# Transposes of a mixer unit's output: offered to later chain steps instead of issued when due

## The chip, the cores and the metric

The kernel runs on one core of a Trainium2 chip. Its time is the device time of one launch in microseconds (us); of several runs the median is given. The engines named here are TensorE (PE in the profile, with its weight loads as PEld), VectorE (DVE), ScalarE (ACT), GpSimd (POOL) and SyncE (SP, which issues most DMAs). Each works through its own instructions in order and waits for the others by semaphores. A matmul writes to PSUM, and VectorE or ScalarE bring its result from there to SBUF.

## The reference

One decoder layer on a sequence of 2048 tokens with 1024 channels: a token mixer with three kinds of heads, then a gated MLP with a short convolution. Cut to what matters here:

```python
def token_mixer(h, w_in, ...):
    proj = h @ w_in
    o_r = retention_chunkwise(rotary(q), rotary(k), v, log_gamma)      # 4 heads
    o_h = gated_state_chunkwise(silu(hq), key_h, hi, log_f)            # 8 heads
    o_a = gated_state_chunkwise(aq, ak, av, g_log)                     # 4 heads
    # each: per-head RMSNorm, times silu of a gate
    o = concatenate([o_r, o_h, o_a]) * head_gain
    return o @ w_out

x = x + g1 * token_mixer(rms_norm(x) * (1 + sc1) + sh1, ...)
x = x + g2 * conv_ffn(rms_norm(x) * (1 + sc2) + sh2, ...)
return rms_norm(x) * final_gain
```

The recurrences are computed by chunks: scores inside a chunk, and a state that is carried from chunk to chunk.

## The kernel before

**Blocks and units.** The sequence is cut into 4 blocks of 512 tokens. In each block the mixer works through 7 units (`ORDER`, L34): h0, g, h1, h2, h3, r0, r1. An h unit is two HGRN2 heads, g is the four GLA heads (it gives two outputs, "first" and "second" below), an r unit is two retention heads. A unit begins with big products that project its inputs (`cf_gemm`, `tf_gemm`, `tf512`). Each is a product in three parts (`split3`, L290): operands are split into a high and a low piece, and three matmuls of up to 512 columns make one step. They fill most of TensorE's time. After that comes the unit's **chain**, a line of small steps, each of which needs what VectorE and ScalarE made of the one before.

**The chain of an h or g unit** (`gated`, L713): dots and the levels 0 and 1 of a tree of scores (L801 to L807), then levels 2 and 3, 4 and 5, and at last 6 alone. Between two pairs the decays are multiplied into q and k (`faded`, on VectorE) and copies are made of them (`ahead`, on ScalarE: `qc`, `kc`). Then: a transpose of k (`kT`, L834), the state's update (`u`, L845), the attention's output (`attn_out`, L857), its normalization and gate (`post`, L639), and, `POST_GAP` (21 us) later, the output's transposes (`transposed`, L652). These are four 128x128 transposes of the unit's output `o` into one PSUM buffer, which ScalarE (L660, the high part) and VectorE (L661, the low part) then read into a tile `oT` for the output projection. For g's second output the gap is 3 us. The chain of a retention unit (`retention`, L988): transposes of q and k and the state's update, scores (L1012 to L1016), the attention's output, the same normalization and transposes.

**What sets the order.** TensorE's order is written out by hand (`manual_schedule`): it is the order in which the Python program emits its instructions. The chains are woven into the big products by a planner (`Clock`, L60), which has a model time `t`. Each emitted product adds its modelled time (`adv`); when `t` passes the due time of a chain's step, that step is emitted at this place. A chain's generator yields the gap in us to its next step; `yield None` lets the next unit's chain begin. `until(done)` (L97) runs due steps one after another, and moves `t` up to their due times, until a condition holds. The program calls it where it can't go on without a result: at L1301, after the first unit of a block, until all eight `oT` of the block before exist, ahead of the second half of that block's output projection (`out_finish`, whose products are `y`); at L1307 for the first four `oT`; and at the mixer's end (L1318, L1322). VectorE's, ScalarE's and SyncE's order is left to a scheduler at build time, by priorities and the order of the program.

**Riders.** A step may yield a pair of times instead of a gap, `(soon, late)` (`RIDE`, L56). From `soon` on it is offered as a rider; the next step that calls `clock.pick()` (L82) emits all riders on offer right behind itself; if none came by `late`, the step is emitted then. Before the change `u` and the attention's output of h and g units and the first part of the statistics for the next block's norm ride. Riders are picked behind the levels 2 and 3, 4 and 5, and 6 (L825), and nowhere else.

**PSUM and SBUF.** Two PSUM buffers, `late_ps` (L155), serve in turn for the dots, `kT`, `u`, the attention's output, `oT` and the norm's statistics (`rstd`). The tiles `a4k` (8 buffers) hold the `oT` and the score matrices; `room(n)` (L231) holds a step back, 1 us at a time, until the planner counts n of them free.

Of the kernel before, what the change touches and what calls it, by code (L numbers as in the profile page):

```python
# [53 lines left out]
FIRST_GAP = 8.0  # L54
PAIR_GAP = (5.2, 6.4)
RIDE = (2.4, 7.4), (3.8, 9.0)  # L56
STAT_GAP, STAT_LAND, NORM_GAP = 2.4, 3.0, 2.0


class Clock:  # L60
# [31 lines left out]
    def adv(self, us):  # L92
        self.t += us
        while self.due and self.due[0][0] <= self.t:
            self._next()
# [29 lines left out]
def trunk(ctx, tc, xT, vecs, cvec, cst, rope, msk, wada, win, walow, wgla, wout, wup, wdown, out):  # L125
# [13 lines left out]
    clock = Clock()  # L139
# [5 lines left out]
    def lev_ps(name):  # L145
        return pp.tile([P, 512], F32, tag="lev", name=name, bufs=2)

    def tiled(out, lhs, rhs, start=True, stop=True):

        for g in range(0, P, 32):  # L150
            T.matmul(out[g:g + 32], lhs[:, g:g + 32], rhs(g) if callable(rhs) else rhs, start=start, stop=stop)
# [3 lines left out]
    def late_ps(name):  # L155
        return pp.tile([P, 512], F32, tag="late", name=name, bufs=2)
# [74 lines left out]
    def room(n):  # L231

        while held[0] + n > NA4:
            yield 1.0
        held[0] += n
# [403 lines left out]
    def post(o, sg, name):  # L639

        o8 = o[:].rearrange("p c (h e) -> p (c h) e", e=64)
        sq = late("osq" + name)
        S.activation(sq[:], o[:].rearrange("p c e -> p (c e)"), AF.Square)
        ms = small("oms" + name)
        V.tensor_reduce(ms[:], sq[:].rearrange("p (a e) -> p a e", e=64), axis=mybir.AxisListType.X, op=ALU.add)
        V.tensor_scalar(ms[:], ms[:], 1.0 / 64, EPS, op0=ALU.mult, op1=ALU.add)
        rs = small("ors" + name)
        newton(ms, rs, 8)
        V.tensor_tensor(o8, o8, rs[:].unsqueeze(2).to_broadcast([P, 8, 64]), op=ALU.mult)
        marked(V.tensor_tensor(o[:], o[:], sg[:], op=ALU.mult))  # L650

    def transposed(b, pos, o, name):  # L652

        ps = late_ps("oT" + name)
        for c in range(NCH):
            T.transpose(ps[:, c * P:(c + 1) * P], o[:, c, :], ident)
        oT = pa.tile([P, 2, TB], F32R, tag="a4k", name="oT" + name)
        g = vec[:, V_HG + pos:V_HG + pos + 1]
        with tc.high_priority(offset=CHAIN):
            S.activation(oT[:, 0, :], ps[:], AF.Copy, scale=g)  # L660
            V.scalar_tensor_tensor(oT[:, 1, :], ps[:], g, oT[:, 0, :], op0=ALU.mult, op1=ALU.subtract)  # L661
        oTs[b][pos] = oT

    def attn_out(name, b, attn, v, qn, W):


        ps = late_ps("o" + name)
        for c in range(NCH):
            oc = ps[:, c * P:(c + 1) * P]
            inter = not (b == 0 and c == 0)  # L670
            if inter:
                tiled(oc, qn[:, c * P:(c + 1) * P], W[:, c, :], stop=False)
            for hh in range(2):
                at, col = attn[hh]
                tiled(oc[:, hh * 64:hh * 64 + 64], at[:, (c * 2 + col) * P:(c * 2 + col + 1) * P],
                      v[:, c, hh * 64:hh * 64 + 64], start=not inter, stop=hh == 1 or not inter)
        return ps

    def carry(b, Sst, ps, decay):

        W = wide.pop(0)
        wide.append(W)
        at = pu.tile([P, NCH - 1, 64], F32, tag="Sc", name="Sc", bufs=2)
        halves = slice(0, 64), slice(64, P)
        if b:
            for rs in halves:
                S.copy(W[rs, 0, rs], Sst[rs, :])
        for c in range(NCH):
            last = c == NCH - 1
            dst, u = Sst[:] if last else at[:, c, :], ps[:, c * 64:c * 64 + 64]  # L690
            if b == 0 and c == 0:
                V.tensor_copy(dst, u)
            elif not last or b < NB - 1:
                V.scalar_tensor_tensor(dst, at[:, c - 1, :] if c else Sst[:], decay(c), u, op0=ALU.mult, op1=ALU.add)
        for rs in halves:
            S.copy(W[rs, 1:NCH, rs], at[rs, :, :])
        return W
# [15 lines left out]
    def gated(name, b, ui, pos, kq, q, decay, subs, qk, sel):  # L713
# [127 lines left out]
        adv(MT)  # L841
        yield RIDE[0]
        ps = late_ps("u" + name)
# [5 lines left out]
        adv(ML)  # L849
        yield RIDE[1]  # L850
        os = []
        for i, (rows, v, sg) in enumerate(subs):
            if i:
                yield RIDE[1]
            o = pu.tile([P, NCH, P], F32, tag="o", name=f"o{name}_{i}")
# [9 lines left out]
        for i, o in enumerate(os):  # L865
            yield POST_GAP if i == 0 else 3.0
            yield from room(1)
            transposed(b, pos + i, o, f"{name}_{i}")
            adv(MT)

# [40 lines left out]
    def unit_g(b, pos):  # L911
# [32 lines left out]
        for i in range(2):  # L944
            rows = [(32 * i, 32 * i + 32), (64 + 32 * i, 96 + 32 * i)]
            for r0, r1 in rows:
                S.copy(q[r0:r1, i, :], qs[r0:r1, :])
            subs.append((rows, *tok_tiles(f"{nm}_{i}")))
        clock.chain(gated(nm, b, 4, pos, kq, q, decay, subs, qk, selg), 12.5)
        pss = tf512(f"vg{nm}", 18)  # L950
        for i in range(2):
# [4 lines left out]
    def unit_r(b, r, pos):  # L956
# [16 lines left out]
        for x, y in zip(a, bb):  # L973
# [10 lines left out]
                        a[1][:].rearrange("p (c h n) -> p c h n", c=NCH, n=64),  # L984
                        kd.unsqueeze(1).unsqueeze(3).to_broadcast([P, NCH, 2, 64]), op=ALU.mult)
        clock.chain(retention(nm, b, r, pos, a[0], kk, kc, q, vsg), 14.5 if b < 3 else 11.0)

    def retention(nm, b, r, pos, a, kk, kc, q, vsg):  # L988
        v, sg = vsg
        Sst = states[5 + r]  # L990
        gc = c_all[:, C_GC + r:C_GC + r + 1]
        qps, kps = lev_ps("qT" + nm), lev_ps("kT" + nm)
        for c in range(NCH):
            T.transpose(qps[:, c * P:(c + 1) * P], a[:, c * P:(c + 1) * P], ident)
        for c in range(NCH):
            T.transpose(kps[:, c * P:(c + 1) * P], kk[:, c, :], ident)
        qn = pu.tile([P, TB], F32, tag="f", name="qn" + nm, bufs=3)
        with tc.high_priority(offset=CHAIN):
            S.copy(kc[:], kps[:])
            S.copy(q[:, 0, :], qps[:])  # L1000
            S.activation(qn[:], qps[:], AF.Copy, scale=gc)
        ps = late_ps("u" + nm)
        for c in range(NCH):
            tiled(ps[:, c * 64:c * 64 + 64], kk[:, c, :], lambda g: v[:, c, g // 64 * 64:g // 64 * 64 + 64])
        with tc.high_priority(offset=CHAIN):
            W = carry(b, Sst, ps, lambda c: gc)
        adv(2 * MT + ML)
        yield 3.5
        yield from room(1)
        at = pa.tile([P, 8 * P], F32, tag="a4k", name="at" + nm)  # L1010
        pss = [lev_ps(f"sc{nm}_{hh}") for hh in range(2)]
        for c in range(NCH):  # L1012
            for g in range(0, P, 32):
                for ps, r0 in zip(pss, (0, 64)):
                    T.matmul(ps[g:g + 32, c * P:(c + 1) * P], kc[r0:r0 + 64, c * P + g:c * P + g + 32],
                             q[r0:r0 + 64, 0, c * P:(c + 1) * P], start=True, stop=True)  # L1016
        with tc.high_priority(offset=CHAIN):
            for hh, ps in enumerate(pss):
                V.tensor_tensor(at[:].rearrange("p (c h n) -> p c h n", c=NCH, h=2)[:, :, hh, :],
                                ps[:].rearrange("p (c n) -> p c n", n=P),  # L1020
                                causal.unsqueeze(1).to_broadcast([P, NCH, P]), op=ALU.mult)
        adv(MS)
        yield 3.0
        ps = attn_out(nm, b, [(at, hh) for hh in range(2)], v, qn, W)
        o = pu.tile([P, NCH, P], F32, tag="o", name="o" + nm)
        qd = c_all[:, C_QD + 2 * r:C_QD + 2 * r + 2]
        with tc.high_priority(offset=CHAIN):
            V.tensor_tensor(o[:].rearrange("p c (h e) -> p c h e", e=64),
                            ps[:].rearrange("p (c h e) -> p c h e", h=2, e=64),
                            qd.unsqueeze(1).unsqueeze(3).to_broadcast([P, NCH, 2, 64]), op=ALU.mult)  # L1030
        with tc.high_priority(offset=AFTER):
            post(o, sg, nm)
        held[0] -= 1
        adv(MO)
        yield None
        yield POST_GAP
        yield from room(1)
        transposed(b, pos, o, nm)
        adv(MT)

# [776 lines left out]
```

## Time and profile before

| | us |
|---|---|
| median of 3 runs (2408.58 to 2411.97) | 2409.89 |
| span of the profiled execution, from its first to its last instruction | 2407.7 |
| TensorE's mean granted clock in it | 0.997 |

The page gives the span of the profiled execution, not its launch time; the runs' median is 2.2 us longer. The mixer's blocks end at about 284, 558, 830 and 1133 us, and the MLP follows to the end.

The output's transposes are 128 matmuls on line 656, in 32 groups of four. Their starts, from the timeline of TensorE, and behind each the start of the next levels 2 to 6 or retention score step on TensorE (us; "behind" says that the group stands right behind another small step):

| unit | block 0 | block 1 | block 2 | block 3 |
|---|---|---|---|---|
| h0 | 138.95, behind a pair of levels | 377.00, 382.26 | 650.58, 654.54 | 922.61, 926.56 |
| g first | 179.37, 181.33 | 451.11, behind o; 458.99 | 725.83, behind o; 733.22 | 997.36, behind o; 1003.38 |
| g second | 183.43, 202.65 | 456.97, 475.07 | 731.21, 748.61 | 1001.42, 1018.50 |
| h1 | 197.98, 202.65 | 476.56, 481.20 | 750.10, 754.74 | 1019.99, 1024.63 |
| h2 | 228.53, 248.76 | 506.49, 521.00 | 780.03, 794.53 | 1049.02, 1057.95 |
| h3 | 266.89, 277.18 | 539.50, 549.29 | 812.86, 822.65 | 1081.31, 1088.08 |
| r0 | 283.59, behind o; 315.09 | 557.24, behind o; 588.73 | 823.74, behind the score | 1086.85, 1088.08 |
| r1 | 305.81, 315.09 | 579.45, 588.73 | 851.48, 860.75 | 1108.43, none |

Here "o" is an attention's output. How a timeline row is read: start in us from the span's beginning, duration, engine, line, operation, output <- inputs by the program's names, shape, and how many instructions were merged; in brackets the idle time before it and what ended it. Matmuls are pipelined, so durations overlap: what an instruction costs is read from starts.

### The profile page before, as it was taken

Reading aid. Unit: us, or ns where it says so; the run is one execution under the profiler, and the core shown is the slowest. Engines: PE = TensorE matmul, PEld = TensorE weight load, DVE = VectorE, ACT = ScalarE, POOL = GpSimd, SP = SyncE. Lnnn points to the kernel's source line nnn. Section 1 sums busy time; section 2 is a strip of 40 time slices with the busy share of each in tenths; the row PEclk is TensorE's granted clock in tenths of the full one; section 3 lists DMA queues with packets and bytes.
Section 4 is the critical chain, followed back from the end, with each engine's and each line's share of the span. In section 5 each row is a group of like instructions: output and inputs, shape, how many; then the busy total and the mean of one; then the engine's idle time right before and its main releaser. Section 6 shows DMA issues by size and latency. Waiting matters only on the chain.

```text
span 2407.7 us, 51890 instructions
## 1 busy us (share of the span) xinstructions
PE 2364.9 (98%) x20523; PEld 1961.5 (81%) x20523; DVE 1818.2 (76%) x3391; ACT 1292.1 (54%) x2311; POOL 153.9 (6%) x275
## 2 busy tenths in 40 slices
PE   7999999999999999999999999999999999999998
PEld 5787878888788888887888888888878888888887
DVE  7687866868577746877988888866888787778566
ACT  4675456744665457644555454554555555455452
POOL 1000100000000100001000000000010100000000
PEclk9999999999999999999999999999999999999999
DMA  7655676797788867788554444687765444548663
GB/s 272 234 187 185 235 262 236 279 330 261 255 305 296 279 203 276 266 280 280 171 172 154 143 158 145 225 282 223 240 198 166 145 149 145 150 151 277 205 198 116
DMA packets 228884, 525.78 MB, mean 218 GB/s; under 512 B 25848, under 2 KB 28832, under 8 KB 228640
## 3 DMA queue, kind: packets, MB, share of 16 engines
q1 hardware_dynamic: 225440, 511.98, 63.7%
q0 software_dynamic: 3200, 10.49, 1.2%
q8 instruction: 161, 2.64, 0.4%
q14 instruction: 83, 0.68, 0.1%
HBM read 392.87 MB, written 129.50 MB: 217 GB/s over the span
## 4 chain that ended last, share of the span: by engine, by line
PE 82%; DVE 8%; DMA 5%; ACT 4%; issue 1%; SPq 0%; DVEq 0%; POOL 0%; ACTq 0%
PE X L292 6%; PE X L294 6%; PE X L293 6%; PE dX L292 4%; PE dX L293 4%; PE dX L294 4%; PE Z L293 3%; PE Z L294 3%; PE Z L292 3%; PE psqkvgr L292 3%; PE psqkvgr L294 2%; PE psqkvgr L293 2%; PE y L292 2%; PE y L293 2%; PE y L294 2%; PE dY L292 2%
## 5 line engine op out<-in xcount | busy, mean ns | idle before, releaser
L293 PE MATMUL X<-B,A 128*128 128x512 f32 x572 | 222.8, 389 | 0.3 <-DVE B L1187 0.3
L292 PE MATMUL X<-B,A 128*128 128x512 f32 x572 | 223.0, 390 | 0.0
L294 PE MATMUL X<-B,A 128*128 128x512 f32 x572 | 222.6, 389 | 0.0
L1187 DVE TENSOR_TENSOR dA<-rd,dA 128x512 fp32r<-128x512 f32 x154 | 106.2, 690 | 91.3 <-ACT dA L1186 91.0
L1186 ACT CAST dA<-rd 128x512 fp32r<-128x512 f32 x154 | 95.6, 622 | 145.7 <-PE dX L294 62.8
L292 PE MATMUL dX<-dB,dA 128*128 128x512 f32 x396 | 154.0, 389 | 0.0
L293 PE MATMUL dX<-dB,dA 128*128 128x512 f32 x396 | 154.0, 389 | 0.0
L294 PE MATMUL dX<-dB,dA 128*128 128x512 f32 x396 | 154.0, 389 | 0.0
L1187 DVE TENSOR_TENSOR A<-s,A 128x512 fp32r<-128x512 f32 x176 | 120.6, 686 | 37.8 <-ACT A L1186 37.7
L1186 ACT CAST A<-s 128x512 fp32r<-128x512 f32 x176 | 108.6, 617 | 60.7 <-PE Z L294 43.5
L292 PE MATMUL psvgh<-hvgh,ha 128*128 128x256 f32 x480 | 139.6, 291 | 0.0
L293 PE MATMUL psvgh<-lvgh,ha 128*128 128x256 f32 x480 | 135.7, 283 | 0.0
L294 PE MATMUL psvgh<-hvgh,ha 128*128 128x256 f32 x480 | 135.6, 283 | 0.0
L293 PEld LDWEIGHTS X<-B,A 128*128 128x128 f32 x572 | 107.4, 188 | 23.2 <-DVE B L1187 1.1
L292 PEld LDWEIGHTS X<-B,A 128*128 128x128 f32 x572 | 107.4, 188 | 22.9 <-ACT u L1493 0.7
L294 PEld LDWEIGHTS X<-B,A 128*128 128x128 f32 x572 | 107.4, 188 | 22.1
L293 PE MATMUL Z<-B,A 128*128 128x512 f32 x308 | 120.6, 392 | 2.3 <-DVE B L1187 2.1
L292 PE MATMUL Z<-B,A 128*128 128x512 f32 x308 | 120.3, 391 | 0.2
L294 PE MATMUL Z<-B,A 128*128 128x512 f32 x308 | 119.9, 389 | 0.0
L1186 ACT CAST A<-r 128x512 fp32r<-128x512 f32 x132 | 82.3, 624 | 63.8 <-PE Z L294 58.2
L1187 DVE TENSOR_TENSOR A<-r,A 128x512 fp32r<-128x512 f32 x132 | 90.6, 687 | 31.3 <-ACT A L1186 30.7
L1187 DVE TENSOR_TENSOR dB<-rb,dB 128x512 fp32r<-128x512 f32 x154 | 105.6, 687 | 7.5 <-ACT dB L1186 7.1
(491 smaller groups left out, 6786.4 us busy)
## 6 DMA issues: line engine op xcount, KB each, us to landing
gs<-yv SPq DMA_DIRECT2D x154, 256.0 KB, 3.0
rb<-gs SPq DMA_DIRECT2D x154, 256.0 KB, 4.3
r<-wup SPq DMA_DIRECT2D x143, 256.0 KB, 3.4
s<-sumsu SPq DMA_DIRECT2D x132, 256.0 KB, 3.2
wada<-wada SPq DMA_DIRECT2D x48, 512.0 KB, 4.5
rd<-sumsd SPq DMA_DIRECT2D x88, 256.0 KB, 4.2
rd<-wdown SPq DMA_DIRECT2D x66, 256.0 KB, 3.9
x<-xT SPq DMA_DIRECT2D x64, 256.0 KB, 5.3
```

The source lines that it names most:

```text
L292: T.matmul(ps, lhs[0], rhs[0], start=first, stop=False, skip_group_check=more)
L293: T.matmul(ps, lhs[0], rhs[1], start=False, stop=False, skip_group_check=more)
L294: T.matmul(ps, lhs[1], rhs[0], start=False, stop=last, skip_group_check=more)
L1186: S.copy(hi, src)
L1187: marked(V.tensor_tensor(lo, src, hi, op=ALU.subtract))
```

## The change

The transposes no longer run when their gap is over: they are offered as riders at once (soon 0.0) and run behind the next step that takes riders, at the latest 7 us after the offer. This holds for h and g units (in `gated`) and for retention units. Behind its score step retention now takes riders too.

```diff
 RIDE = (2.4, 7.4), (3.8, 9.0)
+RIDE_OUT = (0.0, 7.0)
...
         for i, o in enumerate(os):
             yield POST_GAP if i == 0 else 3.0
             yield from room(1)
+            yield RIDE_OUT
             transposed(b, pos + i, o, f"{name}_{i}")
             adv(MT)
...
                                 causal.unsqueeze(1).to_broadcast([P, NCH, P]), op=ALU.mult)
         adv(MS)
+        clock.pick()
         yield 3.0
         ps = attn_out(nm, b, [(at, hh) for hh in range(2)], v, qn, W)
...
         yield None
         yield POST_GAP
         yield from room(1)
+        yield RIDE_OUT
         transposed(b, pos, o, nm)
         adv(MT)
```

## The prediction

> **What bounds the kernel now.** I read the page first (busy time), then the windows by stage, then TensorE's waits, and at last the timeline of TensorE around every group of transposes.
>
> ```profile
> span 2407.7 us, 51890 instructions
> ...
> PE 2364.9 (98%) x20523; PEld 1961.5 (81%) x20523; DVE 1818.2 (76%) x3391; ACT 1292.1 (54%) x2311; POOL 153.9 (6%) x275
> ```
>
> The windows view has busy us by engine (instructions behind each), then the granted clock, the DMA share and GB/s:
>
> ```profile
> 130.00:1115.00 985.00, 970.64 (x13424) 812.51 (x13423) 713.68 (x1774) 562.82 (x1152) 50.42 (x92) 1.00 0.75 262
> 459.00:474.00 15.00, 14.56 (x259) 13.10 (x258) 14.53 (x38) 10.60 (x20) 0.00 (x0) 1.00 0.78 291
> ```
>
> TensorE is the bound: 98% of the span, and in the steady part of the mixer (130 to 1115 us), where the change acts, it sits idle for only 985.00 - 970.64 = 14.4 us. There are two ways to win there: fewer seams between the big split products and the small matmuls, or less of these 14.4 us. The second row warns that VectorE is locally full: 14.53 of 15 us. The rest of the kernel, more than half of it, isn't touched. Three waits stand next to moved transposes (who waited for whom: us in all, times, longest):
>
> ```profile
> PE oTg L656 <- ACT oh L860: 2.8, 2, 1.6
> ...
> PE ssn L151 <- DVE S L694: 2.0, 1, 2.0
> ...
> PE pshfh L292 <- DVE sgg L637: 1.1, 1, 1.1
> ```
>
> **A seam, alone and shared.** Timeline rows are start, duration, instruction. First a pair of levels alone and then a group of transposes alone, both between big products:
>
> ```profile
> 475.35 0.49 PE L768 MATMUL lvh<-qbh,kh 128*32 128x32 f32 x32
> 475.76 0.50 PE L292 MATMUL psqkvgr<-hqkvgr,ha 128*128 128x512 f32 x1
> 476.10 0.39 PE L293 MATMUL psqkvgr<-lqkvgr,ha 128*128 128x512 f32 x1
> 476.33 0.39 PE L294 MATMUL psqkvgr<-hqkvgr,ha 128*128 128x512 f32 x1
> 476.56 0.60 PE L656 MATMUL oTh<-c_all,oh 128*128 128x128 f32 x4
> 476.92 0.48 PE L292 MATMUL psqkvgr<-hqkvgr,ha 128*128 128x512 f32 x1
> 477.23 0.39 PE L293 MATMUL psqkvgr<-lqkvgr,ha 128*128 128x512 f32 x1
> ```
>
> Starts, not durations, are to be compared, since matmuls overlap. A big step is 0.23 us (476.10 to 476.33). The lone transposes put 0.67 us between 476.56 and 477.23 in place of one step: they cost **0.44 us**. Now a group that already stands behind a pair:
>
> ```profile
> 138.54 0.48 PE L768 MATMUL lvh<-qbh,kh 128*32 128x32 f32 x31
> 138.95 0.66 PE L656 MATMUL oTh<-c_all,oh 128*128 128x128 f32 x4
> 139.36 0.47 PE L292 MATMUL pshqh<-ha,hhqh 128*128 128x512 f32 x1
> 139.68 0.39 PE L293 MATMUL pshqh<-ha,hhqh 128*128 128x512 f32 x1
> ```
>
> From the pair's last part to the second big matmul it is 1.14 us here and 0.75 us without a rider (475.35 to 476.10). The rider costs **0.39 us**, so a ride is worth 0.05 us. Seven times more is saved by the riders of before, whose tiles are 32 columns wide. The u step alone, and then behind a pair:
>
> ```profile
> 614.85 0.40 PE L294 MATMUL psakg<-ha,lakg 128*128 128x512 f32 x1
> 615.18 0.65 PE L151 MATMUL uh<-vh,kTh 128*32 128x64 f32 x32
> 615.76 0.50 PE L292 MATMUL psakg<-ha,hakg 128*128 128x512 f32 x1
> 616.10 0.39 PE L293 MATMUL psakg<-ha,hakg 128*128 128x512 f32 x1
> ```
>
> ```profile
> 442.14 0.46 PE L768 MATMUL lvh<-qbh,kh 128*32 128x32 f32 x30
> ...
> 443.01 0.50 PE L292 MATMUL pshfh<-ha,hhfh 128*128 128x512 f32 x1
> ```
>
> Alone: 616.10 - 614.85 less two steps = 0.80. Riding: 443.01 - 442.14 = 0.87 against 0.41 for the pair alone, so 0.46; saved 0.34. The transposes are 128*128 like the big products, and have no such seam of their own to save. The Trainium skill's page "TensorEngine Tiling (Array Packing)", section "Key Properties", says that changing the tiling mode drains the engine. By it a lone group of transposes changes no mode and riding saves nothing, while u and the attention's output save a change; the sum would be 0.6 us higher than by the rows. The rows above agree with it but for 0.05 us.
>
> **Which groups will ride.** From the places of the 32 groups (table in the section on the profile before) and the next step that takes riders: 10 that now stand alone find one within 7 us (unit h0 in blocks 1 to 3, g's first in block 0, h1 in all four, h3 and r0 in block 3). Five stand behind a small step already and will still (h0 in block 0, g's first in blocks 1 to 3, r0 in block 2). The other 17 run out of time. Of these, unit h2's in blocks 1 to 3 should come out next to an attention's output that is due 7 us later, two (r0 in blocks 0 and 1) lose the neighbour they have, and 12 stand alone as before, only later. Thirteen rides won and two lost: 11 x 0.05 = **-0.6 us**. The new taking of riders behind retention's score is worth two of them; no other rider waits there.
>
> **Stalls that go, come or grow.** The o, u, dots, kT, oT and statistics results share two PSUM buffers ("late"). g's second transposes wait 2.8 us in all for a buffer that ScalarE empties late, the statistics 2.0 us for one that VectorE empties late. With g's groups moved to later places and h1's group moved behind the pair at 202.65, another buffer is next, and these 4.8 us can go. Bounds: -4.8 (all) and 0 (VectorE, full in the window at 459 us, is late for the next thing). I take half, **-2.4 us**. In three places the deferred group lands between two other users of these buffers (g's second before the dots of 193.02 and u; h2's between o and u at 513 and 787). Each may wait until ScalarE and VectorE have read what was written 1 to 2 us before: 0 to 1 us each, **+1.5 us**. The wait of 1.1 us at 378.68 ends when VectorE frees a bank; the lone transposes ahead of it cost nothing now, and 0.39 us once they ride: **+0.4 us**.
>
> **What the added wait holds up.** The transposes of r1, the block's last unit, are due just ahead of the loop at L1301, which may not go on to the output projection without them:
>
> ```profile
> 305.81 0.60 PE L656 MATMUL oTr<-c_all,or 128*128 128x128 f32 x4
> ...
> 306.96 0.40 PE L292 MATMUL y<-oTh,hwo 128*128 128x512 f32 x1
> ...
> 308.44 0.43 PE L151 MATMUL dth<-c_all,qkh 128*32 128x2 f32 x32
> ...
> 309.38 0.50 PE L292 MATMUL y<-oTr,hwo 128*128 128x512 f32 x1
> ```
>
> ```profile
> 315.09 0.46 PE L768 MATMUL lvh<-qc,kc 128*32 128x32 f32 x32
> ```
>
> The group runs 1.15 us ahead of the first y. No step that takes riders lies between them, so with the change it is still waiting when the loop is reached. The loop then runs whatever is due until the ticket ends at 305.8 + 7 = 312.8 on the planner's clock: the first pair of the next block's unit h0 (308.44 now), then the transposes. The clock jumps some 6 us without any product in between. The next pair is due 5.2 us behind the first pair on that clock, at about 314.0, so only one or two groups of three y matmuls (0.7 to 1.4 us) and the transposes (0.4 us) are left between the two pairs, where 309.38 to 315.09 = 5.7 us lie now. What the second pair reads is made behind the first one, on VectorE and on ScalarE:
>
> ```profile
> 312.95 0.46 DVE L741 TENSOR_TENSOR kh<-kh,eh 128x256 f32<-128x256 f32 x1
> ```
>
> ```profile
> 311.23 0.62 ACT L751 COPY kc<-kh 128x512 f32<-128x512 f32 x1
> ```
>
> Its first half is ready 311.85 - 309.38 = 2.5 us, its second half 313.41 - 309.38 = 4.0 us behind the first pair, now hidden beneath 5.7 us of y. TensorE reaches the second half 1.4 to 2.1 us behind the first pair, by the count above with 0.28 us for the first half, and runs in order: everything stands behind it. That is a stall of 2.6 to 1.9 us; without an output weight's split on VectorE (1.2 us in this stretch) it could be 0.5, and with the transposes' own two evacuations ahead of the fades some 3.0. I take **1.7 us**. The same happens at two more places; the groups there are
>
> ```profile
> 579.45 0.60 PE L656 MATMUL oTr<-c_all,or 128*128 128x128 f32 x4
> ```
>
> ```profile
> 851.48 0.60 PE L656 MATMUL oTr<-c_all,or 128*128 128x128 f32 x4
> ```
>
> and the distances the same. Three times 1.7 = **+5.1 us** (1.5 to 9). At the mixer's end the loop forces r1's group already now, before its gap is over, so nothing moves there. No DMA moves along with a group: its two evacuations write SBUF only, and SP's and POOL's queues are passed by nothing.
>
> **Sum** against the profiled execution: -0.6 - 2.4 + 1.5 + 0.4 + 5.1 = +4.0, so a span of 2411.7 us. The runs' median, 2409.89, lies 2.2 us above the span, which I take as what lies around it: **2413.9 us**, +0.17%.
>
> **The rivals.** *The seam counts like u's.* If a ride saved 0.34 us, eleven would be -3.7 in place of -0.6; with all 4.8 us of stalls gone and 0.5 us a transition the sum is -3.7 - 4.8 + 1.5 + 0.4 + 1.5 = -5.1: 2404.8. Against it stands the measured rider at 138.95. 7%. *The jump costs more:* the pair behind the loop, at the three block changes. Without it the sum is -1.1 us; from 2.0 us a transition on the kernel is over 0.2% slower. The quoted readiness (4.0 us against 1.4 to 2.1) allows it, and VectorE's extra work there makes it likelier. At 3.0 us it is +7.9: 2417.8. 33%. *The change hardly does what it says:* rides for 15 of 32, and the loop finds the group done because another step took it; then -1.1 us: 2408.8. The order of due times speaks against it, as r1's next taker is 9.3 us off. 10%. My forecast, a jump with its price partly hidden: 50%.
>
> **The numbers.** 0.2%, 4.8 us, is about what a measurement of this kernel can tell from no change. Over that faster: the first rival, 7%, and a little for a chance order of VectorE's work, 9%. Over that slower: 33% and 2% of chance, 35%. Within: 56%. The range reaches from most stalls gone with cheap transitions, 2406.5, to transitions somewhat above 3 us each, 2419.0; the forecast's own is 2410 to 2414.7.
>
> **What would show it.** In the trace of after: 10 to 13 more groups behind a small step, each at 0.39 us in starts; at about 306.5, 580 and 852 us a first pair, transposes, a few y and then the second pair, with a wait on VectorE or ScalarE before it of 1 to 3 us; the oTg and ssn waits smaller. I am wrong if there is no wait at the three places, if riders save 0.3 us each, or if new waits on the two late buffers add up to more than 3 us.

## The result, and the profile after

The changed kernel takes 2433.93 us (median of 4 runs, 2433.09 to 2438.39), the kernel before beside it 2409.69 us (4 runs, 2408.58 to 2411.97). The ratio is 1.010, with a 95% interval of 1.0087 to 1.0114. The forecast was 2413.9 us with a range up to 2419.0: the sign was on record with a chance of 35%, the size was not in the range.

The page of after, its span and the busy time of the engines:

```profile
span 2432.0 us, 51873 instructions
...
PE 2373.5 (98%) x20523; PEld 1966.7 (81%) x20523; DVE 1827.4 (75%) x3391; ACT 1292.3 (53%) x2311; POOL 154.1 (6%) x275
```

TensorE runs as many instructions as before, 20523. Its span is 24.3 us longer. It idles for 2432.0 - 2373.5 = 58.5 us, where it idled for 2407.7 - 2364.9 = 42.8: 15.7 us more. The other 8.6 us are busy time: the same number of matmuls takes longer. So there are two questions: which waits are new, and what slowed the matmuls.

TensorE's waits in after (line, who was waited for: us in all, times, longest):

```profile
PE lvg L769 <- ACT atg L788: 9.0, 6, 3.8
PE ssn L152 <- DVE oTg L662: 6.4, 2, 3.3
...
PE pshfh L293 <- DVE sgg L638: 3.6, 2, 2.5
...
PE ssn L152 <- DVE san L579: 1.7, 1, 1.7
...
PE oTr L657 <- DVE S L695: 1.5, 1, 1.5
```

(Line numbers of after are one to four higher than those of before. `san` is the sum of squares that the statistics `ssn` read, `sgg` the gate of g, `atg` the tiles of g's scores.) The waits on oTg of before, 2.8 us, are gone. In their place stand two larger ones: unit g's last level waits for ScalarE, 9.0 us in all, and the statistics wait for g's second group of transposes, 6.4 us.

The same products, found in both timelines of TensorE, show where the time goes (starts in us):

| first matmul of | before | after | lag |
|---|---|---|---|
| h1's first product, block 1 (pshf) | 378.68 | 379.09 | 0.4 |
| retention's products, block 1 (psqkvgr) | 468.33 | 469.00 | 0.7 |
| next block's h0 (pshf) | 557.65 | 563.02 | 5.4 |
| h1's value product, block 2 (psvgh) | 664.61 | 670.27 | 5.7 |
| h2's forget product, block 2 (pshf) | 677.92 | 692.65 | 14.7 |
| retention's products, block 2 | 742.57 | 751.49 | 8.9 |
| next block's h0 | 829.67 | 846.26 | 16.6 |
| h1's value product, block 3 | 936.63 | 957.13 | 20.5 |
| h2's forget product, block 3 | 949.36 | 975.80 | 26.4 |
| retention's products, block 3 | 1012.73 | 1035.19 | 22.5 |
| an MLP product (X) | 1126.58 | 1150.23 | 23.65 |

A lag that falls again (14.7 to 8.9) means in part that a chain's step stands on the other side of the product, and in part that waits of before are gone: there, pairs of levels waited for `kc` and `kh` at 716.02 and 987.51 us, 3.3 us in all, and in after nothing waits at these pairs. Up to 378.68 us 0.4 us are lost, and behind the last row 0.65 of the 24.3; the rest is lost in the mixer's blocks 1 to 3.

**Place one, predicted: the loop at the block change.** TensorE's timeline of after, the first pair of the new block, r1's transposes, three steps of y and the second pair:

```profile
307.80 0.48 PE L769 MATMUL lvh<-qbh,kh 128*32 128x32 f32 x31
308.21 0.66 PE L657 MATMUL oTr<-c_all,or 128*128 128x128 f32 x4
308.62 0.48 PE L293 MATMUL y<-oTh,hwo 128*128 128x512 f32 x1
308.94 0.40 PE L294 MATMUL y<-oTh,hwo 128*128 128x512 f32 x1
...
310.85 0.46 PE L769 MATMUL lvh<-qc,kc 128*32 128x32 f32 x32
311.64 0.46 PE L769 MATMUL lvh<-qbh,kh 128*32 128x32 f32 x32 [0.33 <-DVE kh L742]
```

The order is the predicted one, and the wait is on the predicted `kh`. But it is 0.33 us here, 0.33 at 590.51 and 0.42 + 0.50 at 872.29: 1.6 us in all, where 5.1 were forecast. The other price of the jump falls some 85 us later.

**Place two: g's last level.** Before, g's levels 4 and 5 stand ahead of unit h1's value product; after, behind its beginning. First before, then after:

```profile
390.53 0.72 PE L768 MATMUL lvg<-qc,kc 64*32 64x32 f32 x62
...
392.33 0.28 PE L292 MATMUL psvgh<-hvgh,ha 128*128 128x256 f32 x1
```

```profile
392.00 0.28 PE L293 MATMUL psvgh<-hvgh,ha 128*128 128x256 f32 x1
...
393.52 0.72 PE L769 MATMUL lvg<-qc,kc 64*32 64x32 f32 x62
```

The product itself came no later; the pair lies 3 us later. By then h1's query work is ahead of g's fades on VectorE. VectorE's timeline, before (`nearg` ahead of `sqh`, h1's query work) and after:

```profile
392.45 0.29 DVE L780 COPY_PREDICATED nearg<-m_all,lvg 128x128 f32<-128x128 uint32 x1
...
399.00 0.69 DVE L886 TENSOR_TENSOR sqh<-pshqh,sqh 128x512 f32<-128x512 f32 x1 [3.71 <-ACT sqh L885]
```

```profile
393.55 0.69 DVE L888 TENSOR_TENSOR sqh<-pshqh,sqh 128x512 f32<-128x512 f32 x1 [0.69 <-ACT sqh L887]
394.27 0.69 DVE L890 TENSOR_TENSOR qkh<-sqh,kh 128x512 f32<-128x512 f32 x1
396.59 1.28 DVE L225 CUSTOM_DVE_ANT_0 wada<-wada,c_act,vec 128x1024 f32<-128x1024 f32 x1 [1.62 <-DMA wada<-wada]
...
398.74 0.49 DVE L781 COPY_PREDICATED nearg<-m_all,lvg 128x128 f32<-128x128 uint32 x2
```

Between the levels and `nearg` stand h1's two products and a reduction that waits 1.62 us for its DMA. ScalarE waits for `nearg` (4.13 us), and only then copies levels 4 and 5 out of PSUM (`atg<-lvg`); the last level writes to the same buffers. ScalarE, before and after:

```profile
392.83 3.33 ACT L791 COPY atg<-nearg 32x256 f32<-32x256 f32 x8 [0.83 <-DVE nearg L780]
```

```profile
399.12 3.32 ACT L792 COPY atg<-nearg 32x256 f32<-32x256 f32 x8 [4.13 <-DVE nearg L781]
402.46 2.15 ACT L788 COPY atg<-lvg 32x128 f32<-32x128 f32 x8
```

The copies start 6.3 us later, and TensorE stands at the last level until they are done: 2.33 + 0.68 us at 403.57, 3.80 + 0.46 at 683.60, 1.09 + 0.68 at 967.47.

**Place three: the statistics.** TensorE, then VectorE, of after:

```profile
474.03 0.60 PE L657 MATMUL oTg<-c_all,og 128*128 128x128 f32 x4
...
475.95 0.65 PE L152 MATMUL uh<-vh,kTh 128*32 128x64 f32 x32
479.72 0.43 PE L152 MATMUL ssn<-c_all,san 128*32 128x1 f32 x32 [3.12 <-DVE oTg L662]
```

```profile
478.33 0.68 DVE L579 TENSOR_TENSOR san<-san,sqn 128x512 f32<-128x512 f32 x1
478.93 0.74 DVE L662 SCALAR_TENSOR_TENSOR oTg<-oTg,vec,oTg 128x512 fp32r<-128x512 f32 x1
```

g's second group ran out its 7 us and now stands just ahead of u and the statistics, three users of two buffers. VectorE reads the group's buffer at 478.93, 4.9 us after the transposes began. The same happens at 761.42 (3.32 us). At the first place the statistics' own input `san` is ready only at 479.01, so even a free buffer would have left 2.4 us of the 3.12; at the second it was ready at 757.97, before the wait began, and the buffer alone held TensorE.

**The clock.** TensorE behind the wait of 3.80 us, and the windows view there (busy us by engine, then the granted clock, DMA share, GB/s):

```profile
683.60 0.63 PE L769 MATMUL lvg<-qbg,kg 64*32 64x128 f32 x2 [3.80 <-ACT atg L788]
684.69 1.10 PE L769 MATMUL lvg<-qbg,kg 64*32 64x128 f32 x30 [0.46 <-ACT atg L788]
...
686.54 0.41 PE L293 MATMUL psvgh<-hvgh,ha 128*128 128x256 f32 x1
686.75 0.41 PE L294 MATMUL psvgh<-lvgh,ha 128*128 128x256 f32 x1
...
690.00 0.28 PE L295 MATMUL psvgh<-hvgh,ha 128*128 128x256 f32 x1
690.12 0.28 PE L293 MATMUL psvgh<-hvgh,ha 128*128 128x256 f32 x1
```

```profile
680.00:684.00 4.00, 0.40 (x2) 0.18 (x2) 1.39 (x2) 3.85 (x12) 0.31 (x1) 0.87 1.01 385
684.00:688.00 4.00, 3.54 (x42) 2.93 (x41) 2.09 (x4) 3.72 (x10) 0.00 (x0) 0.50 0.80 247
688.00:692.00 4.00, 4.00 (x106) 3.87 (x106) 0.67 (x3) 0.69 (x4) 0.00 (x0) 0.78 0.86 298
```

Matmuls of 256 columns start 0.21 us apart at half clock, 0.12 us apart from 690 on. The lost clock is (0.13 + 0.50 + 0.22) x 4 us = 3.4 us. By the same sum over windows of 4 us, the waits at 479.72, 761.42, 942.85 (the 2.5 us on sgg) and 967.47 lose 1.7 us each: 10.2 us in the mixer of after, none in the mixer of before. The prediction has no term for it. The Trainium skill's page "TensorE: Matmul & The Clock Gate", section "Part 1: The HAM clock gate", says that an idle window of about 3.4 us brings half rate, and a busy one full rate again, with windows that run freely. Losses of 1.7 us, what half rate costs in 3.4 us, agree with its length; that waits of 1.8 to 3.3 us were enough does not.

### The profile page after: what moved, and what is told of

Same layout as the page of the kernel before. It is cut to its first block, busy times and chain, and to the rows that moved or that the text cites. A ratio compares the mean times of both kernels' runs of the same rounds, so it can differ in the third digit from the quotient of the medians.

```text
span 2432.0 us, 51873 instructions
## 1 busy us (share of the span) xinstructions
PE 2373.5 (98%) x20523; PEld 1966.7 (81%) x20523; DVE 1827.4 (75%) x3391; ACT 1292.3 (53%) x2311; POOL 154.1 (6%) x275
## 4 chain that ended last, share of the span: by engine, by line
PE 79%; DVE 10%; DMA 5%; ACT 4%; issue 2%; SPq 0%; DVEq 0%; POOL 0%; ACTq 0%
PE X L293 6%; PE X L295 6%; PE X L294 6%; PE dX L294 3%; PE dX L295 3%; PE dX L293 3%; PE Z L294 3%; PE Z L295 3%; PE Z L293 3%; PE psqkvgr L293 2%; PE psqkvgr L295 2%; PE psqkvgr L294 2%; PE psvgh L293 2%; PE psvgh L294 2%; PE psvgh L295 2%
```

## The experiments

All times are medians, ratios are to the kernel before run on the same chip in the same group; a ratio goes by all runs of the group, and differs from the quotient of the two medians by up to 0.15%. Kernels of different groups are compared by their ratios, or by their distance to the kernel before of their own group. Three groups of questions: what the jump costs, what the moved groups cost, what the clock costs. The changed kernel once more in the second group, for comparison:

> The changed kernel once more, beside the kernels it is compared with: 22 to 26 us over the kernel before. Both theories the same.

2438.38 us, ratio 1.011 (1.0095 to 1.0125), as expected. Its trace has the same waits, somewhat shorter at g's last level: 7.7 us there, 6.0 us at the statistics.

### The jump at the loop, alone and taken away

Only the jump, in the kernel before; no group rides or moves:

```diff
             if i == 0 and b:
+                clock.adv(4.6)
                 clock.until(lambda: None not in oTs[b - 1])
```

> The kernel before with no rider added; ahead of the loop at the three block changes the planner's clock is moved by 4.6 us, and nothing else is changed. Theory of the jump: unit g's levels 4 and 5 stand behind the next unit's query products as in the changed kernel, and level 6 waits for the at tiles: 2421 us (2416 to 2428), no wait for the statistics' buffer behind g's transposes. Rival, riders crowd: no rider, no loss: 2411 us.

2422.45 us, ratio 1.0042 (1.0025 to 1.0059). Its timeline of TensorE has the wait at g's last level:

```profile
405.90 0.40 PE L768 MATMUL lvg<-qbg,kg 64*32 64x128 f32 x2 [2.72 <-ACT atg L787]
```

So a move of the planner's clock alone, without a transpose moved, makes place two. The waits there are smaller than after's, though: 5.9 us, of which 3.4 in block 1. The rest stands elsewhere; g's second group, for one, waits 4.9 us for its buffer, where it waited 2.8 before. The whole change with the jump taken away, as the loop runs the waiting group at once:

```diff
             if i == 0 and b:
+                clock.pick()
                 clock.until(lambda: None not in oTs[b - 1])
```

> The changed kernel, but ahead of the loop that waits for the last transposes of a block all riders on offer are run, so that the loop need not move the clock; every group is still deferred. Theory of the jump: as with the h and g units alone, 2417 us (2414 to 2421), no wait for the at tiles of g. Rival, deferral as such (r1's transposes come too late for the output projection, or riders crowd): 2430 us or more, as the changed kernel.

2421.36 us, ratio 1.0039 (1.0026 to 1.0052): more than half of the loss is gone, and no wait at g's last level is over 0.68 us. But of the 6.4 us of place three only 0.6 are left as well, though g's groups still ride, so this run alone doesn't tell the two places apart. The jump kept, but g's chain begun sooner, so that its pairs come back ahead of the product:

```diff
-        clock.chain(gated(nm, b, 4, pos, kq, q, decay, subs, qk, selg), 12.5)
+        clock.chain(gated(nm, b, 4, pos, kq, q, decay, subs, qk, selg), 10.4 if b else 12.5)
```

> The changed kernel with the lead of unit g's chain cut from 12.5 to 10.4 us in blocks 1 to 3: the clock still jumps at the block changes, but g's levels 4 and 5 come ahead of the end of the next unit's query products again, as in the kernel before. Theory of the jump by way of the displaced pair: the long waits for g's at tiles (9.0 us, with a slow clock behind two of them) shrink to under 4 us, and the time falls by 8 to 12 us against the changed kernel: 2421 to 2426 us, if the changed kernel has 2434. Rival (the jump costs by itself, at the block changes, wherever g's pair stands): less than 3 us are won.

2426.22 us, ratio 1.0058 (1.0037 to 1.0078), 12.2 us less than the changed kernel beside it. Of the 9.0 us at the last level 0.9 are left; the statistics' waits (6.5 us) stay. The order of TensorE agrees: level 5's first matmul lies 2.0 to 2.8 us behind the start of h1's value product in blocks 1 to 3 of after, of the jump alone and of retention's riders alone (below), and 0.5 to 1.3 us ahead of it in before, in this run and in the run with the pick. So most of the jump's price comes by way of g's displaced pair; how much of it is paid in waits at the last level differs from run to run.

### Halves of the change

Riders in retention alone (`RIDE_OUT` taken out of `gated`), which keeps the jump:

> Only the retention units' transposes are offered as riders, and the score step takes riders; h and g units' run when due, as before. Theory of the jump: the jump is there at three block changes, the waits for the at tiles of g as in the changed kernel (9 us and the slow clock behind), none for the statistics' buffer behind g's transposes: 2423 us (2418 to 2428). Rival, riders crowd: few riders are left, so near the kernel before: 2411 us.

2423.2 us, ratio 1.0043 (1.0028 to 1.0058), as the jump alone. The time is the expected one, the waits aren't: 3.7 us at g's last level in place of 9, and 2.8 us on `sgg` at 658.58 and 4.7 us of g's second group on its buffer, which the expectation had not named. So the number was met in part by luck. Then riders in `gated` alone, without a jump:

> Only h and g units' transposes are offered as riders; a retention unit's run when due, as before. Theory of the jump (the loop ahead of the output projection moves the planner's clock some 5 us when it has to wait out r1's ticket; unit h0's chain then runs early and pushes unit g's levels 4 and 5 behind the next unit's query work on VectorE and ScalarE): no jump, so the waits of 9.0 us for the at tiles of g and of 2.5 us at the h products of block 3 go, with the slow clock behind the longest of them; the waits of 6.4 us for the statistics' buffer stay. 2417 us (2414 to 2421). Rival, riders crowd (the evacuations of transposes that ride behind a pair of levels delay what the next pair reads): all the h and g riders are still there, so the waits for the at tiles stay: 2430 or more.

2425.43 us, ratio 1.005 (1.0034 to 1.0065). Neither theory had put it there: without the jump half of the loss was still to be found. Nor did the waits of 6.4 us for the statistics' buffer stay, as was expected; in their place `u` waits 2.17 us for `nearh`, a tile that VectorE writes. It was split again, by `if not two:` and `if two:` ahead of `yield RIDE_OUT` in `gated`.

> Only the h units' groups ride; g's two groups and retention's run when due, so the loop at the block change does not jump. Theory late buffers (the loss of the run without retention's riders, +12.8 us, comes from g's two groups, which then stand between other users of the two late buffers): 2410 to 2415 us, no wait on oTg or nearh over 1.5 us. Rival theory h groups (the h groups, seven microseconds later, shift the chains themselves): 2420 us or more.

> Only g's two groups ride. Theory late buffers: most of the +12.8 us is here, 2420 to 2426 us, with waits of 2 us or more at kT, u or ssn in blocks 1 and 2. Rival theory h groups: within 3 us of the kernel before, 2409 to 2415.

The h units alone: 2421.45 us, ratio 1.004 (1.0025 to 1.0055). g alone: 2418.97 us, 1.0033 (1.0021 to 1.0044). Both lose, so the account that it is all g's buffers falls. In the run with g alone the two waits at the statistics are there as in after (3.16 and 3.32 us), without a jump and without any other group moved: place three is made by g's groups. In the run with the h units alone the statistics wait for `san`, not for a group:

```profile
199.02 0.39 PE L295 MATMUL psqkvgr<-hqkvgr,ha 128*128 128x512 f32 x1
201.58 0.55 PE L152 MATMUL ssn<-c_all,san 128*32 128x1 f32 x32 [2.17 <-DVE san L579]
...
203.11 0.63 PE L293 MATMUL psqkvgr<-hqkvgr,ha 128*128 128x512 f32 x1
203.54 0.63 PE L294 MATMUL psqkvgr<-lqkvgr,ha 128*128 128x512 f32 x1
```

A big step behind it takes 0.43 us in place of 0.23: here a wait of 2.17 us brought half clock.

### g's second group, and both repairs

The second group run when due, as before the change (`if i == 0:` ahead of `yield RIDE_OUT` in `gated`):

> The changed kernel, but g's second transposes run when due, 3 us behind the first, and are no riders. Theory of the two late buffers (the deferred second group stands just ahead of u and the statistics, which then must have its buffer while ScalarE and VectorE still read it): the statistics' waits of 3.1 and 3.3 us and the slow clock behind both go, 9 to 10 us in all if nothing takes their place; some of it comes back as the wait of 1.2 to 1.7 us that the second group had before. 7 us won against the changed kernel (5 to 9). Rival (VectorE is full there, and the wait moves to the next thing that needs it): less than 3 us.

2433.28 us, ratio 1.0084 (1.0068 to 1.0099), 5.1 us won, the least that was expected. The wait in block 1 did not go but changed its releaser (3.48 us at 483.81, on `san`); the one in block 2 fell from 3.32 to 1.19 us, also on `san`. With the pick at the loop as well:

> Both repairs: riders are run ahead of the loop at the block changes, so the clock doesn't jump, and g's second transposes aren't deferred. If the two mechanisms are all there is: within 2 us of the kernel before. If riders crowd ScalarE and VectorE elsewhere too: 5 us or more over it.

2431.16 us, ratio 1.0077 (1.0062 to 1.0092): worse by far than the pick alone. The two repairs don't add up, and the trace has a wait that neither kernel had, `kTh` on a group's buffer:

```profile
PE kTh L835 <- DVE oTg L662: 4.5, 1, 4.5
```

### Moving the groups without riding

The kernel before, with the groups of h and g units due 4 us later, and in another run 2 us sooner. No group of transposes rides, and the clock does not jump:

```diff
-            yield POST_GAP if i == 0 else 3.0
+            yield POST_GAP + 4.0 if i == 0 else 3.0
```

> The kernel before, without any riders for these groups; the groups of h and g units are due 25 us behind the attention's output in place of 21. Theory place (what costs is that these groups stand elsewhere between the other users of the two late buffers and in the order of VectorE and ScalarE, riding or not): 6 to 14 us slower than before, 2418 to 2426, like the run without retention's riders. Rival theory riding (the cost is in standing behind another small step, which crowds VectorE there): within 3 us of before, 2410 to 2415.

> The kernel before; the groups of h and g units are due 19 us behind the attention's output in place of 21. Theory place: a shift of 2 us costs something too, 3 us or more, 2415 to 2424. Rival theory riding: within 3 us of before, 2410 to 2415. Should the order of before be no special one, a shift could as well win: below 2409.

Later: 2426.54 us, ratio 1.0059 (1.0042 to 1.0075). Sooner: 2424.25 us, 1.005 (1.0035 to 1.0065). A shift to either side costs 12 to 15 us (each just above the range that the theory of the place had named), as much as the riders of h and g units, 12.8: so riding isn't needed for a loss of this size, another place is enough. Each trace has a long wait at one of the late buffers. TensorE of the later run, then TensorE and VectorE of the sooner one:

```profile
463.34 0.66 PE L834 MATMUL kTh<-c_all,kh 128*128 128x128 f32 x4 [3.84 <-ACT oh L860]
```

```profile
475.53 0.66 PE L656 MATMUL oTh<-c_all,oh 128*128 128x128 f32 x4
481.32 0.60 PE L151 MATMUL ssn<-c_all,san 128*32 128x1 f32 x32 [5.13 <-DVE oTh L661]
```

```profile
479.72 0.69 DVE L1069 TENSOR_TENSOR wsu<-wsu,wsu 128x512 f32<-128x512 f32 x1
...
480.51 0.75 DVE L661 SCALAR_TENSOR_TENSOR oTh<-oTh,vec,oTh 128x512 fp32r<-128x512 f32 x1
```

In the sooner run h1's group meets the statistics, and VectorE, without a gap between 475.9 and 481.2, reads the group 5 us after it ran. Would a lead for the evacuations mend it? Three kernels got it:

```diff
-        with tc.high_priority(offset=CHAIN):
+        with tc.high_priority(offset=2 * CHAIN):
             S.activation(oT[:, 0, :], ps[:], AF.Copy, scale=g)
```

> The changed kernel; the two evacuations of every group get twice the lead in the order of VectorE and ScalarE, so that they go ahead of the chains' own work. Theory late evacuation (a moved group costs because its buffer is read late in a full VectorE): the two waits of the statistics for oTg, 6.0 to 6.5 us in all, fall below 3 us, and the kernel is 4 to 8 us faster than the changed one, 2426 to 2430, with half clock at these places gone. Rival theory full VectorE (whoever goes first, another is as late; g_second went that way): the waits move to san, nearh or the levels and the kernel stays within 3 us of the changed one, 2431 to 2437.

> The kernel before with the same lead for the evacuations. Theory late evacuation: its own waits for such buffers are short (2.8 us on oTg come from another evacuation), so 2408 to 2414, no change. Rival theory full VectorE, and any other order than that of before costs: 3 us or more slower, 2415 to 2425.

> The run with the riders picked ahead of the loop (2421.4 us), with the same lead for the evacuations. Theory late evacuation: another 2 to 5 us, 2416 to 2420. Rival theory full VectorE: within 3 us, 2418 to 2425, or slower.

The changed kernel: 2433.39 us, ratio 1.0069 (1.0052 to 1.0086). The kernel before: 2412.86, 0.9997 (0.9983 to 1.0011). The pick at the loop: 2420.86, 1.0029 (1.0019 to 1.0038). The two waits on oTg stay (6.1 us), since VectorE's order at that place hardly moved: `L662` still starts at 478.75, behind both `san`. The lead didn't do what it was to do, so whether an earlier evacuation would repair the loss stays open. By its ratio the changed kernel with the lead looks better than without (1.0069 against 1.010 and 1.011 in other groups), but its trace lies as far behind before's at the MLP product of the table (24.2 us against 23.65 and 22.6): a difference of this size between ratios of two groups says little.

### The clock

The changed kernel with work in TensorE's idle time: matmuls into a free buffer, read by nobody, ahead of g's last level in blocks 1 to 3.

```diff
+            if two and b and not pair_:
+                keep_going(acc_ps(f"idle{name}"), 12)
             if pair_:
                 level(li, True)
```

> The changed kernel, with twelve matmuls of 256 columns whose result nobody reads ahead of g's last level in blocks 1 to 3, so that TensorE works while it would wait there (about 1.3 us of work at each place). Theory slow clock (a part of the loss is the half clock after the waits at 683.6 and 967.5): the granted clock stays near 1 at these two places and the kernel is 3 to 5 us faster than the changed one, about 2430. Rival theory (only idle time counts, the clock is a by-product): 2433 to 2437, no faster, as the filling takes only idle time and costs up to 1 us where there is none.

2445.0 us, ratio 1.0134 (1.0117 to 1.015): a miss, in the main because a filling matmul took 0.44 us, so that twelve took 5.34 us at each place, more than the idle time. Filling that fits:

```diff
+            n = {2: 8, 3: 3}.get(b, 0) if two and not pair_ else 0
+            if n:
+                keep_going(acc_ps(f"idle{name}"), n)
```

> The changed kernel with filling that fits the idle time, since a filling matmul took 0.44 us and not 0.11: eight (3.55 us) ahead of g's last level in block 2, where TensorE idled for 4.26 us, and three (1.33 us) in block 3, where it idled for 1.77; none in block 1, where the clock did not fall. Theory slow clock: the granted clock stays near 1 at both places, and from the second head product of block 2 to the forget product of unit h1 the lag behind the kernel before grows by 5 to 7 us in place of 9.1, in block 3 by 4 to 5 in place of 5.9; in all 4 to 5 us faster than the changed kernel, 2428 to 2431. Rival theory (only idle time counts): 8.5 to 9.5 and 5.5 to 6.5 us of growth, 2433 to 2436 in all.

2427.95 us, ratio 1.0069 (1.0052 to 1.0085), the ratio of the run with the lead, though 11 matmuls more run. The changed kernel wasn't run beside it, and the filled kernel's trace is 2 us ahead of after's at h1's first product of block 1 already, before any filling; so the total shows little, and the places themselves must. TensorE and a window of that run:

```profile
679.24 3.61 PE L425 MATMUL idleg<-c_all 128*128 128x256 f32 x16
682.78 1.13 PE L769 MATMUL lvg<-qbg,kg 64*32 64x128 f32 x32
```

```profile
684.00:688.00 4.00, 4.00 (x74) 3.87 (x77) 2.65 (x5) 2.66 (x8) 0.00 (x0) 1.00 0.75 243
```

The level starts as soon as ScalarE lets it, and the clock stays at 1.00 where it was 0.50. From h1's value product to h2's forget product (the expectation says h1 for h2) the lag grows by 6.8 us in block 2, in place of 9.1 in after. The changed kernel's second trace lies between: it idled 3.62 us there, lost 1.7 us of clock, and its lag grew by 8.3; in the run with the lead, with waits of 2.88 + 0.68 us, it grew by 7.8. So the filling won 1.0 to 2.2 us in block 2.

In block 3 the lag grows by 4.5 us in place of 5.9, but not for the filling: the second trace of the changed kernel, with no filling, grows by 4.5 too. It has the same waits as after there, 1.09 + 0.68 us, and yet its clock didn't fall. Windows behind these waits, in after and in the second trace:

```profile
968.00:972.00 4.00, 3.44 (x45) 3.25 (x46) 2.41 (x5) 3.67 (x9) 0.00 (x0) 0.71 0.85 285
```

```profile
968.00:972.00 4.00, 3.57 (x54) 3.37 (x55) 2.53 (x5) 3.54 (x9) 0.00 (x0) 1.00 1.00 284
```

Same kernel, same waits, half clock in one execution and not in the other, and 1.5 us between them: the slow clock is a loss of its own, beside the idle time. In block 1, unfilled, the clock fell in the filled run (0.66 in the window at 400 us) behind a shorter wait than after's.

## Why the prediction was wrong, step by step

- **TensorE is the bound, and VectorE is locally full.** Right; the second half decides more than it was given weight.
- **Riding saves 0.05 us each, -0.6 us.** The price was right, the count in part by luck. 19 of 32 groups stand behind a small step, 7 before: 12 more, where a net 11 were counted. Of the thirteen rides forecast ten came; h0's in blocks 1 to 3 did not, and r1's three at the loop and g's second in block 0, which had been counted as standing alone, did. A rider costs 308.94 - 307.80 = 1.14 us with the pair's last part, the figure of before to the hundredth.
- **The jump, +5.1 us.** This step failed. Its mechanism was right (order, tile and line of the wait), but its price was put at the next pair, 1.6 us in all, and followed no further. The jump also moved every later due time against the products: g's levels 4 and 5 came behind the start of h1's value product some 85 us later, and VectorE's and ScalarE's order there cost 9.0 us of waits and, with the clock, up to 5.1 more. The run with g's chain begun sooner puts the price of this displacement at 12.2 us. The signs named for the trace failed here too: waits of 1 to 3 us were forecast, and 0.3, 0.3 and 0.9 came. The rival that gave the slower outcome its 33% put the price at the same pair, with 2.0 us a transition as the point that decides; so the sign that it had came true for another reason.
- **Stalls that go, -2.4, and new waits on the late buffers, +1.5.** The first was near: oTg's 2.8 us went; the statistics' 2.0 became 1.7 us on another releaser. The second was mis-sized: 6.4 us at the two places where g's second group meets u and the statistics, with 3.4 us of clock. At the first of the two the buffer added only 0.7 us to the wait for `san`. The sign of being wrong, more than 3 us of such waits, came true. The three places that I had priced at 0 to 1 us each show no wait; the two that do have the statistics as the buffer's next user, which I had left out. A stall that the list had left out went as well: the 3.3 us on `kc` and `kh`.
- **The wait at 378.68, +0.4 us.** It didn't come: h0's group found no rider's place and ran alone at 381.23.
- **Not in the sum at all:** 2.5 us at 942.85 on sgg and 1.5 at 840.35, and the granted clock. New waits and lost clock, less the stalls that went, come to 9.0 + 5.1 + 6.4 + 3.4 + 1.6 + 2.5 + 1.7 + 1.5 - 2.8 - 0.3 - 0.6 = 27.5 us; less the 3.3 us on `kc` and `kh` it is 24.2, where the span grew by 24.3. That it comes out so close is luck: waits under 1 us are left out on both sides, and the clock's terms are upper bounds, as a part of the slow time is idle (10.2 us of clock, 8.6 us of busy time).
- **What stays open.** With the jump gone some 0.3 to 0.4% remain, and the runs that move groups without riding lose as much or more. The runs show that moving the groups is enough for a loss, and that long waits at the late buffers come with it in the run with g alone and in both shifts; how much of each loss these waits make isn't shown, and no run shows a repair that takes it away. No version ran measurably faster than the kernel before.

## What to carry to other kernels

Where engines work through an order fixed beforehand, a moved step must be followed past its own neighbours: find what each later product and chain step now stands ahead of, for the whole block, before pricing anything. Count for each shared buffer its next two users and ask when a full engine will read it; a group that can stand anywhere on TensorE may not be able to on VectorE. And allow for a new wait of some 2 us on TensorE to cost more than its own length: half clock behind it took 1.5 us in one execution of a kernel here, and nothing in the next. Last, compare two small losses only where the kernels ran side by side.

## What the hardware showed beside

Half clock came behind waits of 2.5 us (942.85), 1.09 + 0.68 us (967.47) and, in another run, 2.17 us (201.58), but not behind 2.33 + 0.68 us (403.57). In the changed kernel's second trace it was the other way about: half clock behind 1.60 + 0.68 us (402.06), none behind 1.09 + 0.68 us (967.35). The length of a wait alone doesn't decide. In after it cost 1.7 us of clock each time, once 3.4. Filling an idle stretch of 4.26 us with 3.55 us of useless matmuls kept the clock at 1.00 and won 1.0 to 2.2 us at that place, against three traces without it.
